# A decoder trunk in split float32: operand starts at one remainder by 256 bytes, and a gate projection in columns of 512, 512 and 320

## The chip, the core and the metric

The kernel runs on one core of a Trainium2 chip. The metric is the time of one execution on the device in microseconds (us). Each kernel is run several times, and the median is compared. Beside the runs one execution is profiled; its trace gives every instruction's start, and the views quoted here come from it.

## What is computed

The reference is a trunk of two layers over 256 tokens of width 1024, all in float32. Each layer is a half-step SwiGLU FFN, a token mixer and a second half-step FFN, each with a norm before and after. The mixer of the first layer is a gated linear recurrence (RG-LRU), that of the second is attention with a forget gate. Keys, values and forget gates come from the stream between the two layers.

```python
D_MODEL, SEQ, D_FF, D_RNN = 1024, 256, 2816, 1344

def swiglu(x, w_gate, w_up, w_down):
    return (jax.nn.silu(x @ w_gate) * (x @ w_up)) @ w_down

def recurrent_block(x, w_in, conv_w, conv_b, w_a, b_a, w_x, b_x, lam, w_out):
    gx = x @ w_in
    gate, rec = gx[..., :D_RNN], gx[..., D_RNN:]
    rec = causal_depthwise_conv(rec, conv_w, conv_b)
    rec = rg_lru(rec, w_a, b_a, w_x, b_x, lam)
    return (jax.nn.gelu(gate) * rec) @ w_out

for layer in range(2):
    if layer == 1:
        k, v, c = shared_kv(h, kv_norm_g, w_kv, w_f, b_f)     # c: running sum of the forget gates' logs
    h = h + 0.5 * rms_norm(swiglu(rms_norm(h, ...), ...), ...)
    h = h + rms_norm(recurrent_block(...) if layer == 0 else forgetting_attention(...), ...)
    h = h + 0.5 * rms_norm(swiglu(rms_norm(h, ...), ...), ...)
```

## The kernel before

**Products.** Each float32 product is made of three: both operands are split into an upper part (`whi`, `xhi`: a rounded copy) and a lower part (`wlo`, `xlo`: the rest), and `mm3` (lines 181 to 183) issues upper with upper, upper with lower, lower with upper into one accumulator. In `mm3` the tokens stand still (128 x 128, loaded into the array) and the weights move past them, up to 512 columns at a time. The 256 tokens are two halves of 128, called t = 0 and 1.

**Weights.** They come in units of up to 1024 numbers per partition. A unit is loaded into one of five `raw` tiles, split by ScalarE (`whi`, L171) and VectorE (`wlo`, L175) into one of nine pairs of tiles, and used by both halves. A unit of a projection holds two or more blocks of 128 input rows side by side: block j begins at column j times nn of the tile, nn being the width of its column group. So where a block begins in memory depends on nn.

**Stages and order.** The stages are: FFN 1 of layer 0, the recurrent mixer, FFN 2 of layer 0, keys and values together with FFN 1 of layer 1, attention, FFN 2 of layer 1. TensorE's instructions keep the order in which the program writes them: lists of units that `run` walks through for both halves, and a written-out order for the mixer (`RG_ORDER`) and the attention (`ATT_ORDER`). The other engines' instructions are ordered by a scheduler from priorities and estimated costs, except where `keep_in_program_order` holds one. `tick`, called after each unit, prepares units ahead by a planner's clock (`pace`, which counts columns) and works off deferred steps.

**FFN.** Gate and up projections have column groups of 512 (five) and 256 (one of each, in one unit). Their product, `prod`, is transposed on TensorE (L508) and split into `hhi` and `hlo`, tiles of 22 x 128 numbers per half, which are the standing operand of the down projection: 22 blocks of 128 rows, two groups of 512 columns.

**The mixer's gate.** The gate half of `w_in`, 1344 columns, is computed with the tokens standing, in three column groups (`GCOLS`): 504, 504 and 336. The groups follow the recurrence's tiles of 126 channels, four tiles to a group. `add_gate_unit` makes the units: four of two blocks each for the first two groups, three of up to three blocks for the third. When a group is complete for a half, an activation takes it out of the accumulator into a `tok` tile (L644 with the gelu at once for the first, L646 as a copy for the others); four `tok` buffers serve the six pieces in turn. `batch` later applies the gelu to the copied pieces (L800), and `gate_T` transposes them by tiles of 126 channels (L818), four tiles of group g for batch g.

**Memory.** Tiles lie in pools, which stand one behind the other in each partition's memory. A tile begins at a multiple of 32 bytes. The pools `const`, `w`, `h` and `small` stay for the whole program, and in them every `raw`, `whi`, `wlo`, `xhi` and `xlo` tile begins at a remainder of 160 by 256. Behind them lie in turn: `rgw` and the first FFN's pool `ffn_a` (160); `rgw` and the mixer's pool `rg` (160); and from the second FFN on the pool `kv`, which begins at byte 147,616 (160) and stays, with `ffn_b`, then `att`, then `ffn_c` behind it, each from byte 174,944 (96). The FFN's tiles `sil`, `prod`, `hhi` and `hlo`, and the attention's `oh` and `ol`, have sizes that are multiples of 256 bytes, so they all have their pool's remainder. `zhi` and `zlo`, the normed tokens of keys and values, lie in the place of `hhi` and `hlo`.

The functions that the change touches and their callers follow.

Of the kernel before, what the change touches and what calls it, by code (L numbers as in the profile page):

```python
# [9 lines left out]
F32 = mybir.dt.float32  # L10
F32R = mybir.dt.float32r
BF16 = mybir.dt.bfloat16
AF = mybir.ActivationFunctionType
# [3 lines left out]
P = 128  # L17
# [3 lines left out]
DRNN = 1344  # L21
BLK = 84
RT = 126
NRT = 11
NH = 16
# [14 lines left out]
def width(i):  # L40
    return RT if i < 10 else BLK
# [3 lines left out]
def trunk_kernel(ctx: ExitStack, tc: tile.TileContext, A: dict, out: bass.AP):  # L45
    nc = tc.nc
# [11 lines left out]
    def nm(s):  # L58
        uid[0] += 1
        return f"{s}_{uid[0]}"  # L60

    def mmbank():
        return psum.tile([P, 512], F32, tag="mm", name=nm("mm"), bufs=4)
# [4 lines left out]
    def trbank():  # L68
        return psum.tile([P, 512], F32, tag="tr", name=nm("tr"), bufs=2)
# [71 lines left out]
    def main_x(t, k):  # L141
        return xhi[:, k, t * P:(t + 1) * P], xlo[:, k, t * P:(t + 1) * P]
# [11 lines left out]
    def load_raw(src, parts, n, pieces=1):  # L154
        v = new_raw()[:parts, :n]
        if len(src.shape) == 3:
            a, m = src.shape[1] // pieces, n // pieces
            for c in range(pieces):
                nc.sync.dma_start(v[:, c * m:(c + 1) * m].rearrange("p (a b) -> p a b", a=a),
                                  src[:, c * a:(c + 1) * a, :])  # L160
        else:
            nc.sync.dma_start(v, src)
        return v

    def split(rawv, parts, n, pieces=1, pin=False):
        u = Unit()
        hi = wpool.tile([P, 1024], F32R, tag="whi", name=nm("whi"), bufs=WB)
        lo = wpool.tile([P, 1024], F32R, tag="wlo", name=nm("wlo"), bufs=WB)
        m = n // pieces
        for c in range(0, n, m):  # L170
            up = nc.scalar.activation(hi[:parts, c:c + m], rawv[:, c:c + m], AF.Copy)  # L171
            if settled[0] or pin:
                tc.keep_in_program_order(up)
                settled[0] = False
            nc.vector.tensor_tensor(lo[:parts, c:c + m], rawv[:, c:c + m], hi[:parts, c:c + m].bitcast(F32), ALU.subtract)  # L175
        u.hi, u.lo = hi[:parts, :n], lo[:parts, :n]
        return u

    def mm3(ps, xh, xl, wh, wl, first, last):
        tensor_work(3 * wh.shape[1])  # L180
        nc.tensor.matmul(ps, xh, wh, start=first, stop=False)  # L181
        nc.tensor.matmul(ps, xh, wl, start=False, stop=False)  # L182
        nc.tensor.matmul(ps, xl, wh, start=False, stop=last)  # L183
# [358 lines left out]
    pools = {}  # L542
# [71 lines left out]
    n_ffn1 = len(items)  # L614


    GCOLS = [(0, 4 * RT), (4 * RT, 4 * RT), (8 * RT, 2 * RT + BLK)]
    rg = {}

    def w_in(c0, n, k0, kn):  # L620
        return A["rg_w_in"][0, k0 * P:(k0 + kn) * P, c0:c0 + n].rearrange("(k p) n -> p k n", p=P)

    gacc = {}
    toks = {}
    plain = []
    xcs, tt, th, yy = {}, {}, {}, {}

    def add_gate_unit(g, k0, kn):
        c0, nn = GCOLS[g]

        def prep():
            return split(load_raw(w_in(c0, nn, k0, kn), P, kn * nn), P, kn * nn)

        def work(t, u):
            if k0 == 0:
                gacc[(g, t)] = mmbank()
            ps = gacc[(g, t)][:, :nn]
            for j in range(kn):
                k = k0 + j
                mm3(ps, *main_x(t, k), u.hi[:, j * nn:(j + 1) * nn], u.lo[:, j * nn:(j + 1) * nn], k == 0, k == 7)  # L640
            if k0 + kn == 8:
                tok = toks[(g, t)] = pools["r"].tile([P, 4 * RT], F32, tag="tok", name=nm("tok"), bufs=4)
                if (g, t) == (0, 0):
                    nc.scalar.activation(tok[:, :nn], ps, AF.Gelu_apprx_tanh)  # L644
                else:
                    nc.scalar.activation(tok[:, :nn], ps, AF.Copy)  # L646
                    plain.append(tok[:, :nn])
        rg[f"g{sum(n[0] == 'g' and n[1] != 'w' for n in rg)}"] = len(items)
        items.append((prep, work))

    def tiles_of(p):
        return [2 * p, 2 * p + 1] if p < 5 else [10]

    def pw(p):
        return RT if p < 5 else BLK
# [133 lines left out]
    def batch(g):  # L789

        pairs = [p for p in (2 * g, 2 * g + 1)]
        tps, ys = {}, {}

        def roots():
            for (a, b, w) in parts_of(g):
                v = tt[g][:w, a:b, :]
                nc.scalar.activation(v, v, AF.Sqrt)
            while plain:
                v = plain.pop(0)
                tc.keep_in_program_order(nc.scalar.activation(v, v, AF.Gelu_apprx_tanh))  # L800

        def u_of(p):
            w, m = pw(p), len(tiles_of(p))
            v = tt[g][:w, 2 * (p % 2):2 * (p % 2) + m, :]
            nc.vector.scalar_tensor_tensor(v, th[p][1][:w, :m, :], -1.0, v, ALU.mult, ALU.mult)
            nc.vector.tensor_tensor(v, v, xcs[p][:w, :m, :], ALU.mult)

        def scan(p, j):
            w = pw(p)
            v = tt[g][:w, 2 * (p % 2) + j, :]  # L810
            nc.vector.tensor_tensor_scan(v, th[p][0][:w, j, :], v, 0.0, ALU.mult, ALU.add)

        def gate_T(t):
            tok = toks[(g, t)]
            tp = tps[t] = trbank()
            for j in range(len(pairs) * 2 if g < 2 else 3):
                w = width(4 * g + j)
                nc.tensor.transpose(tp[:w, j * P:(j + 1) * P], tok[:, j * RT:j * RT + w], ident)  # L818

        def product(t):  # L820
            y = ys[t] = pools["r"].tile([RT, 4, P], F32, tag="y", name=nm("y"), bufs=2)
            if t == 0:
                yy[g] = [rw.tile([P, 1024], F32R, tag="gy", name=nm("y"), bufs=6).rearrange("p (t a b) -> p t a b", t=2, a=4)
                         for _ in range(2)]
            for (a, b, w) in parts_of(g):
                tp = tps[t][:w, a * P:b * P].rearrange("p (a b) -> p a b", a=b - a)
                nc.vector.tensor_tensor(y[:w, a:b, :], tp, tt[g][:w, a:b, t * P:(t + 1) * P], ALU.mult)
                nc.scalar.activation(yy[g][0][:w, t, a:b, :], y[:w, a:b, :], AF.Copy)

        def low(t):  # L830
            yh, yl = yy[g]
            for (a, b, w) in parts_of(g):
                nc.vector.tensor_tensor(yl[:w, t, a:b, :], ys[t][:w, a:b, :], yh[:w, t, a:b, :].bitcast(F32), ALU.subtract)

        key = ("y", g)
        q = [(0.0, key, roots)]
        for p in pairs:
            s = len(tiles_of(p)) / 2
            q.append((1.3 * s, key, lambda p=p: u_of(p)))
            q += [(0.72, key, lambda p=p, j=j: scan(p, j)) for j in range(len(tiles_of(p)))]  # L840
        q.append((0.0, key, lambda: (gate_T(0), gate_T(1))))
        for t in range(2):
            q.append((0.7, key, lambda t=t: product(t)))
        for t in range(2):
            q.append((0.7, key, lambda t=t: low(t)))
        queue.extend(q)

    def parts_of(g):
        return [(0, 4, RT)] if g < 2 else [(0, 2, RT), (2, 3, BLK)]
# [35 lines left out]
    kv = {}  # L885
# [10 lines left out]
    def kv_tiles():  # L896
        lp = ctx.enter_context(tc.tile_pool(name="kv", bufs=1, reuse_waits="tile"))
        kv["kT"] = lp.tile([HA, NH, S], F32, name="kT")
        kv["v"] = [lp.tile([P, D], F32, name=f"v{t}") for t in range(2)]
        kv["lf"] = [lp.tile([P, NH], F32, name=f"lf{t}") for t in range(2)]  # L900
        kv["c"] = [lp.tile([NH, P], F32, name=f"c{t}") for t in range(2)]
        kv["bfb"] = lp.tile([P, NH], F32, name="bfb")
        for n in ("triu", "mone", "cmask"):
            kv[n] = lp.tile([P, P], F32, name=n)
# [353 lines left out]
    rw_cm.__exit__(None, None, None)  # L1258

    kv_tiles()  # L1260
    defer(20, kv_constants)
    fcm = open_pool("f", "ffn_b")
# [57 lines left out]
```

## Time and profile before

| | us |
|---|---|
| median of 3 runs | 995.11 (994.96 to 995.67) |
| the profiled execution | 994.69 |
| its span, first to last instruction | 993.0 |
| TensorE busy in it | 984.4 (99%) |
| VectorE busy | 618.5 (62%) |
| ScalarE busy | 530.5 (53%) |

The page of the profile has the busy time of each engine, the chain of work that ended last, and groups of instructions by line. The list of waits says which engine waited for what. The timeline lists instructions with their start, their length in us, engine, line, and the operands as out<-moving,standing. The windows give, for stretches of the span, their length, TensorE's busy time and count, the granted share of TensorE's clock, and the share and rate of the DMA engines. TensorE's instructions overlap: the length in a row is longer than the distance to the next start.

### The profile page before, as it was taken

How to read it: one execution, taken by the hardware profiler on the slowest of the kernel's cores; microseconds unless marked ns; L12 is line 12 of the kernel's file. 1: busy time of each engine (PE TensorE's matmuls, PEld its weight loads, DVE VectorE, ACT ScalarE, POOL GpSimd, SP SyncE). 2: the span in 40 equal slices, each digit the busy share in tenths (PEclk: the TensorE clock that was granted, in tenths of full speed). 3: DMA queues.
4: the chain of work that ended last, by engine and by line, in shares of the span. 5: the costliest groups of instructions: out<-in, count | busy, mean ns of one | idle time of the engine just before them, and what ended most of it. 6: DMA issues, size and time to landing. Idle time of an engine off the chain costs nothing.

```text
span 993.0 us, 12910 instructions
## 1 busy us (share of the span) xinstructions
PE 984.4 (99%) x4776; PEld 816.9 (82%) x4776; DVE 618.5 (62%) x792; ACT 530.5 (53%) x752; POOL 47.0 (5%) x92
## 2 busy tenths in 40 slices
PE   9999999999999999999999999999999999999997
PEld 6888888898988888888898888888888788888886
DVE  6756554668997555554686655554488876555542
ACT  7545443568886544443564444444366765444431
POOL 2400000100003000000100000000020000000000
PEclk9999999999999999999999999999999999999999
DMA  8967556465346766555567666655542467665531
GB/s 287 310 192 206 189 190 190 150 199 160 119 132 190 217 182 191 191 182 188 131 199 237 175 187 190 190 173 190 188 172 64 126 195 212 189 189 191 182 116 42
DMA packets 92645, 178.89 MB, mean 180 GB/s; under 512 B 11966, under 2 KB 32614, under 8 KB 92582
## 3 DMA queue, kind: packets, MB, share of 16 engines
q1 hardware_dynamic: 90998, 176.89, 58.0%
q10 hardware_dynamic: 752, 1.06, 0.3%
q8 instruction: 37, 0.61, 0.3%
q0 software_dynamic: 832, 0.12, 0.1%
q14 instruction: 26, 0.21, 0.1%
HBM read 176.95 MB, written 1.05 MB: 179 GB/s over the span
## 4 chain that ended last, share of the span: by engine, by line
PE 97%; issue 1%; DMA 1%; DVE 1%; ACT 0%; POOL 0%; POOLq 0%; DVEq 0%; ACTq 0%
PE mm L181 29%; PE mm L183 29%; PE mm L182 28%; PE tr L508 2%; PE gt L739 2%; PE gt L1040 1%; PE mm L188 1%; PE mm L190 1%; PE mm L189 1%; PE mm L1169 1%; PE mm L1075 1%; DMA raw<-in_ffn_w_gate_dram 1%; PE tr L1061 1%; PE gt L212 1%; PE tr L936 0%
## 5 line engine op out<-in xcount | busy, mean ns | idle before, releaser
L175 DVE TENSOR_TENSOR wlo<-raw,whi 128x1024 fp32r<-128x1024 f32 (+4 forms) x329 | 395.7, 1208 | 271.5 <-ACT whi L171 270.9
L171 ACT ACTIVATE whi<-raw 128x1024 fp32r<-128x1024 f32 (+4 forms) x329 | 341.8, 1045 | 317.1 <-PE mm L183 253.8
L181 PE MATMUL mm<-whi,xhi 128*128 128x512 f32 (+2 forms) x768 | 303.7, 395 | 0.0
L183 PE MATMUL mm<-whi,xlo 128*128 128x512 f32 (+2 forms) x768 | 298.9, 389 | 0.3 <-DVE xlo L226 0.3
L182 PE MATMUL mm<-wlo,xhi 128*128 128x512 f32 (+2 forms) x768 | 298.1, 388 | 0.0
L183 PEld LDWEIGHTS mm<-whi,xlo 128*128 128x128 f32 x768 | 144.2, 188 | 31.0 <-DVE xlo L226 0.7
L181 PEld LDWEIGHTS mm<-whi,xhi 128*128 128x128 f32 x768 | 144.3, 188 | 28.7 <-issue 1.3
L182 PEld LDWEIGHTS mm<-wlo,xhi 128*128 128x128 f32 x768 | 144.5, 188 | 27.9 <-DVE wlo L175 0.3
L181 PE MATMUL mm<-whi,hhi 128*128 128x512 f32 x352 | 138.2, 393 | 0.0
L183 PE MATMUL mm<-whi,hlo 128*128 128x512 f32 x352 | 138.0, 392 | 0.0
L182 PE MATMUL mm<-wlo,hhi 128*128 128x512 f32 x352 | 137.5, 391 | 0.0
L182 PEld LDWEIGHTS mm<-wlo,hhi 128*128 128x128 f32 x352 | 66.1, 188 | 14.3
L183 PEld LDWEIGHTS mm<-whi,hlo 128*128 128x128 f32 x352 | 66.1, 188 | 14.0
L181 PEld LDWEIGHTS mm<-whi,hhi 128*128 128x128 f32 x352 | 66.1, 188 | 13.8
L502 DVE SCALAR_TENSOR_TENSOR prod<-mm,rstd,sil 128x512 f32<-128x512 f32 (+1 forms) x48 | 33.9, 706 | 37.7 <-PE mm L183 34.0
L493 ACT ACTIVATE sil<-mm,rstd 128x512 f32<-128x512 f32 (+1 forms) x48 | 31.2, 652 | 40.6 <-PE mm L183 40.5
L196 POOL TENSOR_SCALAR nv<-ss 128x1 f32<-128x1 f32 x22 | 9.5, 432 | 722.2 <-ACT junk L203 722.2
L512 ACT ACTIVATE hhi<-tr 128x512 fp32r<-128x512 f32 (+1 forms) x48 | 26.6, 554 | 15.4 <-PE tr L508 15.3
L203 ACT ACTIVATE junk<-mm 128x512 bf16<-128x512 f32 x24 | 14.3, 597 | 32.9 <-PE mm L183 32.8
L270 DVE TENSOR_TENSOR t<-mm,gb 128x512 f32<-128x512 f32 x24 | 16.2, 689 | 24.9 <-ACT junk L203 24.8
L513 DVE TENSOR_TENSOR hlo<-tr,hhi 128x512 fp32r<-128x512 f32 (+1 forms) x48 | 30.5, 643 | 1.4
L181 PE MATMUL mm<-whi,zhi 128*128 128x340 f32 (+2 forms) x80 | 28.3, 354 | 0.0
(195 smaller groups left out, 898.0 us busy)
## 6 DMA issues: line engine op xcount, KB each, us to landing
raw<-in_ffn_w_down_dram SPq DMA_DIRECT2D x88, 512.0 KB
raw<-in_ffn_w_up_dram SPq DMA_DIRECT2D x80, 512.0 KB
raw<-in_ffn_w_gate_dram SPq DMA_DIRECT2D x78, 512.0 KB
raw<-in_rg_w_in_dram SPq DMA_DIRECT2D x20, 504.0 KB
raw<-in_rg_w_out_dram SPq DMA_DIRECT2D x10, 504.0 KB
raw<-in_ffn_w_gate_dram SPq DMA_DIRECT2D x18, 256.0 KB
raw<-in_ffn_w_up_dram SPq DMA_DIRECT2D x16, 256.0 KB
raw<-in_w_kv_dram SPq DMA_DIRECT2D x8, 512.0 KB
```

Of the source, the lines that this page charges most:

```text
L171: up = nc.scalar.activation(hi[:parts, c:c + m], rawv[:, c:c + m], AF.Copy)
L175: nc.vector.tensor_tensor(lo[:parts, c:c + m], rawv[:, c:c + m], hi[:parts, c:c + m].bitcast(F32), ALU.subtract)
L181: nc.tensor.matmul(ps, xh, wh, start=first, stop=False)
L182: nc.tensor.matmul(ps, xh, wl, start=False, stop=False)
L183: nc.tensor.matmul(ps, xl, wh, start=False, stop=last)
L270: nc.vector.tensor_tensor(t1[n], pf[n], gb[:, n * 512:(n + 1) * 512], ALU.mult)
L493: nc.scalar.activation(s[:, :nn], ps, AF.Silu, scale=rs[t][:, 0:1])
L502: nc.vector.scalar_tensor_tensor(pr[:, :nn], ps, rs[t][:, 0:1], s, ALU.mult, ALU.mult)
L508: nc.tensor.transpose(tp[:, j * P:(j + 1) * P], pr[:, j * P:(j + 1) * P], ident)
L512: nc.scalar.activation(hv, tp[:, :nn], AF.Copy)
L513: nc.vector.tensor_tensor(lv, tp[:, :nn], hv.bitcast(F32), ALU.subtract)
L739: nc.tensor.matmul(ps[j][:w, g * S:(g + 1) * S], wv[rows, o:o + w], xc[rows, k, :], start=start, stop=stop, skip_group_check=True)
```

## The change

Three edits. The gate's column groups become 512, 512 and 320. A half's gate tokens are held in one tile of 1344 columns, of which the pieces are slices, and `gate_T` reads batch g's channels from column 504 g of it; there is one such tile for each half, `tok0` and `tok1`, in place of four buffers. And the two tiles `lf` of the pool `kv` are allocated with 8 more columns, which are not used: 96 bytes instead of 64 each, so that the pools behind `kv` begin 64 bytes later.

```diff
-    GCOLS = [(0, 4 * RT), (4 * RT, 4 * RT), (8 * RT, 2 * RT + BLK)]
+    GCOLS = [(0, 512), (512, 512), (1024, DRNN - 1024)]
...
             if k0 + kn == 8:
-                tok = toks[(g, t)] = pools["r"].tile([P, 4 * RT], F32, tag="tok", name=nm("tok"), bufs=4)
+                if t not in toks:
+                    toks[t] = pools["r"].tile([P, DRNN], F32, name=f"tok{t}")
+                tok = toks[t][:, c0:c0 + nn]
                 if (g, t) == (0, 0):
-                    nc.scalar.activation(tok[:, :nn], ps, AF.Gelu_apprx_tanh)
+                    nc.scalar.activation(tok, ps, AF.Gelu_apprx_tanh)
                 else:
-                    nc.scalar.activation(tok[:, :nn], ps, AF.Copy)
-                    plain.append(tok[:, :nn])
+                    nc.scalar.activation(tok, ps, AF.Copy)
+                    plain.append(tok)
...
         def gate_T(t):
-            tok = toks[(g, t)]
+            tok = toks[t][:, 4 * g * RT:]
...
-        kv["lf"] = [lp.tile([P, NH], F32, name=f"lf{t}") for t in range(2)]
+        kv["lf"] = [lp.tile([P, NH + 8], F32, name=f"lf{t}")[:, :NH] for t in range(2)]
```

## The prediction

> **What bounds the kernel now.** I read the page first (span, the chain of waits), then TensorE's waits, then the timeline of single products in stretches where nothing but products runs, and last the windows over those stretches with their counts.
>
> ```profile
> span 993.0 us, 12910 instructions
> PE 97%; issue 1%; DMA 1%; DVE 1%; ACT 0%; POOL 0%; POOLq 0%; DVEq 0%; ACTq 0%
> ```
>
> ```profile
> PE mm L1169 <- DVE whi L1136: 0.9, 1, 0.9
> PE tr L125 <- PEq L1305: 0.8, 1, 0.8
> PE mm L183 <- DVE xlo L226: 0.3, 1, 0.3
> PE gt L739 <- issue: 0.3, 1, 0.3
> PE mm L1169 <- ACT whi L1138: 0.2, 1, 0.2
> ```
>
> The chain of what ended last is TensorE for 97%, and TensorE's list of waits holds 2.5 us in all, 1.9 of it in the first stretch of the program (L125 and L1169 are its opening lines). So the end is set by how fast TensorE steps from one product to the next. A busy time of "0.39" in the rows below is a modelled latency: the pace is the distance from one start to the next.
>
> Here are two down projections, each in one of the stretches where only products run: the first FFN, then the second.
>
> ```profile
> 147.11 0.39 PE L181 MATMUL mm<-whi,hhi 128*128 128x512 f32 x1
> 147.34 0.39 PE L182 MATMUL mm<-wlo,hhi 128*128 128x512 f32 x1
> 147.57 0.39 PE L183 MATMUL mm<-whi,hlo 128*128 128x512 f32 x1
> 147.79 0.39 PE L181 MATMUL mm<-whi,hhi 128*128 128x512 f32 x1
> ```
>
> ```profile
> 446.32 0.39 PE L181 MATMUL mm<-whi,hhi 128*128 128x512 f32 x1
> 446.55 0.39 PE L182 MATMUL mm<-wlo,hhi 128*128 128x512 f32 x1
> 446.77 0.39 PE L183 MATMUL mm<-whi,hlo 128*128 128x512 f32 x1
> 447.01 0.39 PE L181 MATMUL mm<-whi,hhi 128*128 128x512 f32 x1
> ```
>
> The same three products, in the same shapes, take 0.68 us in the first FFN and 0.69 in the second. Whole stretches with their counts make that firm. The rows are the four down projections in order, each from its last transposes to its end (the count holds three instructions too many in each, the tail of what ran just before):
>
> ```profile
> 140.89:191.31 50.42, 50.42 (x225) 1.00 0.51 156
> 439.36:487.51 48.15, 48.15 (x213) 1.00 0.55 165
> 674.63:722.77 48.14, 48.14 (x213) 1.00 0.54 175
> 933.06:986.46 53.40, 53.40 (x236) 1.00 0.30 99
> ```
>
> 50.42 / 222 = 227.1 ns for one product in the first; 48.15 / 210 = 229.3, 48.14 / 210 = 229.2 and 53.40 / 233 = 229.2 in the others. The granted clock is 1.00 in all four. The DMA share (0.51, 0.55, 0.54, 0.30) does not order them: the last has the least traffic and the slow pace.
>
> What does order them is where the operands lie. Adding up tile sizes in the order of the pools, all weight tiles, xhi and xlo begin at remainder 160 (bytes, modulo 256). The pool of the first FFN does so too, and its hhi and hlo are whole multiples of 256 long: 160 against 160. The pool `kv` begins at 160 and holds 16384 + 2 x 4096 + 2 x 64 + 2 x 512 + 64 + 3 x 512 bytes, which is 106 x 256 + 192. So every pool opened after it begins at 96: hhi, hlo, zhi, zlo, oh, ol and their like of the later stages lie at 96 while the moving weights lie at 160.
>
> **The change part by part.** I work against the profiled execution, 994.69 us (span 993.0 and 1.69 around it); the median of the runs shown, 995.11, is 0.42 above it, and I add that at the end.
>
> *The padding of lf.* Two tiles grow from 64 to 96 bytes, so the later pools begin 64 bytes on, at 160. No instruction is added. A down projection has 22 x 2 x 2 x 3 = 264 products; three of the four move from 96 to 160: 792 x (229.25 - 227.1) = 1.70 us less. The other products with a stationary operand at 96 are the K projection (L181 to L183 with zhi, zlo) and the output projection of the attention (oh, ol), 96 products each:
>
> ```profile
> 538.53 0.47 PE L181 MATMUL mm<-whi,zhi 128*128 128x512 f32 x1
> 548.23 0.38 PE L936 MATMUL tr<-ident,htok 128*128 128x128 f32 x2
> 562.30 0.48 PE L181 MATMUL mm<-whi,xhi 128*128 128x512 f32 x1
> 571.93 0.49 PE L508 MATMUL tr<-ident,prod 128*128 128x128 f32 x3
> 795.18 0.39 PE L182 MATMUL mm<-wlo,oh 128*128 128x512 f32 x1
> 800.45 0.39 PE L181 MATMUL mm<-whi,xhi 128*128 128x512 f32 x1
> 805.91 0.27 PE L212 MATMUL gt<-ident,h 128*128 128x128 f32 x1
> ```
>
> Between 538.53 and 548.23 lie 42 products with z: 231.0 ns each, against 229.3 for the 42 products with x (160 against 160) from 562.30 to 571.93, which also begin behind transposes. That is 1.7 x 96 = 0.16 us. The 23 products with oh and ol up to 800.45 take 229.1 each, the 24 with x that follow without a break 227.5: 1.6 x 96 = 0.15 us. The V projection has 144 products of width 360 and 340, whose second slots stay at other remainders: I take nothing, bounds 144 x 2.15 = 0.3 either way. The float32 products (gates, logits, values; 122 in the code) change remainder as well, and no row shows one of them at two: nothing, bounds 122 x 2.15 = 0.3 either way.
>
> *Gate columns 512, 512, 320.* The column sum stays 1344 and so does the count of products: 96 of 504 become 512, 48 of 336 become 320. A second slot at 504 columns lies 2016 bytes on, at remainder 128; at 512 it lies at 160 again, and 320 columns are 5 x 256 bytes.
>
> ```profile
> 206.89 0.39 PE L181 MATMUL mm<-whi,xhi 128*128 128x504 f32 x1
> 209.64 0.28 PE L188 MATMUL mm<-xhi,whi 128*126 128x256 f32 x1
> 249.74 0.32 PE L183 MATMUL mm<-whi,xlo 128*128 128x336 f32 x1
> 253.14 1.03 PE L818 MATMUL tr<-ident,tok 128*126 128x128 f32 x8
> 254.14 0.28 PE L189 MATMUL mm<-xlo,whi 128*126 128x256 f32 x1
> 259.65 0.60 PE L739 MATMUL gt<-xc,gw 126*126 126x256 f32 x2
> ```
>
> Twelve products of 504 take 2.75 us, 229.2 each: more than the 227.1 of an aligned 512. By that row a wider product is 2.1 ns cheaper: 96 x 2.1 = 0.20 less. By width alone it would be dearer: 22 products of 336 take 3.40 us, 154.5 each, so a column costs (227.1 - 154.5) / 176 = 0.41 ns, and 8 columns 96 x 3.3 = 0.32 more. I take the first, since the row is of this very product; both are bounds. For 320 I have neighbours on both sides: 47 products of 256 in 5.51 us are 117.2 each, so the slope below 336 is 37.3 / 80 = 0.47. Sixteen columns less are 6.6 to 7.5 ns: 48 x 7 = 0.34 less.
>
> The Trainium skill ("TensorE: Matmul & The Clock Gate", section "Back-to-back issue gap") gives a warm gap of N / 2.4 + 2.5 ns, from the width alone. By it 504 to 512 would cost 0.32 us, 336 to 320 would return the same, and the padding would change nothing. The four windows above disagree: one width, one clock, 227.1 and 229.2.
>
> *One tile for a half's tokens.* Six pieces in four buffers become slices of two tiles, 10,752 bytes instead of 8,064; the later pools still end below the row's end. The three pieces of a half are written by the same number of activations, and the transposes read 126 columns from the slice as before. A piece of the third group no longer waits for a buffer to come free. The loads carry the same bytes in rows of 2048 and 1280 instead of 2016 and 1344; TensorE's waits name no DMA in this stage, so I cost them at nothing. If that cover were gone, a late split would show as a wait on whi or wlo; the list has none there. The splits become 1024 and 960 elements wide for 1008, on engines that are not the bound. Nothing is queued behind a new wait unless the shared tile makes one (second rival).
>
> Sum: 1.70 + 0.16 + 0.15 + 0.20 + 0.34 = 2.55 us less. 994.69 - 2.55 = 992.1 profiled, 992.5 as a median. Nothing stands ready to take the place of this time: TensorE waits for nobody between 10 and 986 us but 0.3 us twice.
>
> **The rivals.** *Width alone.* The pace goes by the width, and the slow pace of the later stages has another cause (their neighbours, their traffic). Then the padding gives nothing and the columns +0.32 - 0.34: 995.1, no change. For it: only one down projection of four is aligned, so one stage could differ for reasons of its own. Against it: oh and x in one unbroken run, one width, 229.1 and 227.5; and 504 dearer than 512. The skill's rule above is this rival's formula.
>
> *A wait on the shared tile (the slower side).* A read of one slice of a tok tile waits for the last write to any slice of it. The transposes (L818) stand in TensorE's order right behind the products of the third group, whose copy (L646) comes later on ACT:
>
> ```profile
> 255.59 0.43 ACT L646 ACTIVATE tok<-mm 128x336 f32<-128x336 f32 x1
> 272.11 1.03 PE L818 MATMUL tr<-ident,tok 128*126 128x128 f32 x8
> 273.57 0.46 ACT L646 ACTIVATE tok<-mm 128x336 f32<-128x336 f32 x1
> ```
>
> The first eight transposes start at 253.14 and would wait until 256.02, 2.9 us; the next eight at 272.11 until 274.03, 1.9 us. TensorE's order is fixed, so all products behind them wait too: +4.8 - 2.55 = +2.3, 997.4. It decides from the point where the waits together exceed 2.55. Against it, the program already writes and reads two halves of one tile at once:
>
> ```profile
> 203.99 2.17 ACT L244 ACTIVATE xhi<-gt,gT 128x128 fp32r<-128x128 f32 x8
> 204.38 0.39 PE L182 MATMUL mm<-wlo,xhi 128*128 128x504 f32 x1
> 205.16 2.16 DVE L247 SCALAR_TENSOR_TENSOR xlo<-gt,gT,xhi 128x128 fp32r<-128x128 f32 x8 [0.41 <-ACT xhi L244]
> ```
>
> ACT writes the second half's columns of xhi until 206.16 and DVE those of xlo until 207.32, while TensorE reads the first half's at 204.38 without waiting. So waits go by the bytes touched.
>
> **How the numbers follow.** Forecast 0.81, width alone 0.10, shared tile 0.09. The forecast's own bounds: at worst 1.70 + 0.34 with nothing from z and oh, 0.32 lost on the 504s, 0.3 on V and 0.3 on float32, 1.1 less, 994.0; at best 2.55 + 0.3 + 0.3, 3.15 less, 992.0. With the 0.7 us over which the three runs shown are spread (994.96 to 995.67), half to each side and a little more: 991.3 to 994.3, which leaves out the two rivals and hardly anything else. About 0.2%, 2.0 us, is what a measurement of this kernel can tell from no change. Of the forecast's share I put 0.70 beyond that and 0.11 within it; with width alone, 0.21 within; 0.09 slower.
>
> **What would show it.** Right: the windows over the second to fourth down projections give about 227.1 ns for one product, as the first did; three products take 0.68 us; each of these stages is 264 x 2.15 = 0.57 us shorter; the gate's 512-wide products step at about 227 and the 320-wide at 147; TensorE's waits stay at about 2.5 us. Wrong: the later down projections still at 229 (width alone); the transposes at L818 with an idle gap ended by ACT tok (shared tile); a new wait on whi or wlo from the gate units on, which would say that the order on ACT and DVE has shifted.

## The result and the profile after

The changed kernel takes 992.52 us (median of 8 runs, 992.08 to 993.69) against 994.87 (8 runs): ratio 0.9976, 95% interval 0.9966 to 0.9986. It is faster by 2.35 us. Its profiled execution took 992.08.

The page of the changed kernel, span and chain of waits, and below it TensorE's list of waits (us in total, times, longest):

```profile
span 990.4 us, 12910 instructions
PE 97%; issue 1%; DMA 1%; DVE 1%; ACT 0%; POOL 0%; POOLq 0%; DVEq 0%; ACTq 0%
```

```profile
PE tr L125 <- PEq L1309: 0.8, 1, 0.8
PE gt L742 <- issue: 0.5, 1, 0.5
PE mm L1173 <- ACT whi L1142: 0.3, 1, 0.3
PE mm L183 <- DVE xlo L226: 0.3, 1, 0.3
```

The same number of instructions, the same bound, no new wait on an operand. What moved is the pace. The windows over the four down projections of the changed kernel, in order; the count again holds three instructions too many:

```profile
140.68:191.10 50.42, 50.42 (x225) 1.00 0.48 157
438.80:486.53 47.73, 47.73 (x213) 1.00 0.54 167
673.20:720.92 47.72, 47.72 (x213) 1.00 0.54 176
930.93:983.87 52.94, 52.94 (x236) 1.00 0.29 100
```

The first is as long as before, 50.42 us or 227.1 ns a product. The others are 47.73 / 210 = 227.3, 47.72 / 210 = 227.2 and 52.94 / 233 = 227.2, where they had 229.2 to 229.3. The gate's rows that answer to those of the prediction (timeline):

```profile
206.72 0.39 PE L181 MATMUL mm<-whi,xhi 128*128 128x512 f32 x1
209.45 0.28 PE L188 MATMUL mm<-xhi,whi 128*126 128x256 f32 x1
249.48 0.31 PE L183 MATMUL mm<-whi,xlo 128*128 128x320 f32 x1
252.71 0.49 PE L821 MATMUL tr<-ident,tok 128*126 128x128 f32 x3
```

Twelve products of 512 columns take 2.73 us (227.5 by these rows; 2.75 before), and 22 of 320 take 3.23 (146.8 each; 3.40 before).

Summed over all products of a stage, from start to start, in the two profiled executions (us):

| | before | after | difference | predicted |
|---|---|---|---|---|
| down projections, all four | 242.03 | 240.47 | -1.56 | -1.70 |
| gate, 504 to 512 | 22.46 | 22.54 | +0.08 | -0.20 |
| gate, 336 to 320 | 7.53 | 7.14 | -0.39 | -0.34 |
| K projection | 22.33 | 22.24 | -0.09 | -0.16 |
| attention's output projection | 23.30 | 23.22 | -0.08 | -0.15 |
| V projection | 23.11 | 23.00 | -0.11 | 0 |
| other products with x, after the opening | 489.09 | 488.71 | -0.38 | 0 |
| transposes of the gate's tokens | 2.68 | 2.85 | +0.17 | 0 |
| opening, from TensorE's first instruction to its 115th | 27.22 | 27.05 | -0.17 | 0 |

The last row matters for all comparisons below. The opening varies from run to run by more than some of the effects (27.05 to 30.33 us over the kernels of this study): by the waits for the first operands, and by the pace of its first products, which the last section shows. "Outside the opening" means the span less that stretch: 965.76 before, 963.32 after, 2.44 us less.

### The profile page after: what moved, and what is told of

Its sections match the earlier page's. It is cut to its first block, busy times and chain, and to the rows that moved or that the text cites. A ratio compares the mean times of both kernels' runs of the same rounds, so it can differ in the third digit from the quotient of the medians.

```text
span 990.4 us, 12910 instructions
## 1 busy us (share of the span) xinstructions
PE 982.4 (99%) x4776; PEld 816.5 (82%) x4776; DVE 618.6 (62%) x792; ACT 530.2 (54%) x752; POOL 47.1 (5%) x92
## 4 chain that ended last, share of the span: by engine, by line
PE 97%; issue 1%; DMA 1%; DVE 1%; ACT 0%; POOL 0%; POOLq 0%; DVEq 0%; ACTq 0%
PE mm L181 29%; PE mm L183 28%; PE mm L182 28%; PE tr L508 2%; PE gt L742 2%; PE gt L1044 1%; PE mm L188 1%; PE mm L189 1%; PE mm L190 1%; PE mm L1173 1%; PE mm L1079 1%; PE tr L1065 1%; PE gt L212 1%; DMA raw<-in_ffn_w_gate_dram 1%; PE tr L940 0%
## 5 line engine op out<-in xcount | busy, mean ns | idle before, releaser
L175 DVE TENSOR_TENSOR wlo<-raw,whi 128x1024 fp32r<-128x1024 f32 (+5 forms) x329 | 395.6, 1207 | 270.1 <-ACT whi L171 267.1
L171 ACT ACTIVATE whi<-raw 128x1024 fp32r<-128x1024 f32 (+5 forms) x329 | 341.8, 1045 | 315.5 <-PE mm L183 250.6
L181 PE MATMUL mm<-whi,xhi 128*128 128x512 f32 (+1 forms) x768 | 303.5, 395 | 0.0
L183 PE MATMUL mm<-whi,xlo 128*128 128x512 f32 (+1 forms) x768 | 298.9, 389 | 0.3 <-DVE xlo L226 0.3
L182 PE MATMUL mm<-wlo,xhi 128*128 128x512 f32 (+1 forms) x768 | 298.4, 388 | 0.0
```

## The experiments

Throughout, D is the remainder by 256 of the standing operand's start less that of the moving operand's start, in the products of `mm3`. Ratios are to the kernel before. Before, D was 0 for x and for the first FFN's hidden tokens, and -64 for the standing operands of the later stages, each against the first block of a unit; further blocks of the narrower groups stood elsewhere (the gate's second blocks of 504 columns at D = +32).

**The parts alone.** First the padding without the rest:

```diff
 (the kernel before)
-        kv["lf"] = [lp.tile([P, NH], F32, name=f"lf{t}") for t in range(2)]
+        kv["lf"] = [lp.tile([P, NH + 8], F32, name=f"lf{t}")[:, :NH] for t in range(2)]
```

> Padding of lf alone, columns and token tiles as before. Theory (the start of the standing operand against that of the moving one, modulo 256, sets the pace): the later three down projections step at 227.2 to 227.3 ns as in the changed kernel, and the time is 1.8 us below before (1.56 down projections, 0.1 each for K, V and the attention's output projection): ratio 0.9982. Rival (pace by width alone, the gain of the change lies in the gate's columns): no difference, ratio 1.000, down projections still at 229.2.

Measured: 992.56 us, ratio 0.9975 (0.9966 to 0.9985). Its windows over the second and fourth down projection:

```profile
439.32:487.05 47.73, 47.73 (x213) 1.00 0.56 167
931.38:984.32 52.94, 52.94 (x236) 1.00 0.31 100
```

The pace of the changed kernel, 227.3 and 227.2, with columns and token tiles untouched. Outside the opening it is 963.48, 2.28 us below before, where 1.8 was expected; 0.31 of it lies in products with x, which were not in that sum. So nearly the whole gain is the padding.

Then the rest without the padding:

```diff
 (the changed kernel)
-        kv["lf"] = [lp.tile([P, NH + 8], F32, name=f"lf{t}")[:, :NH] for t in range(2)]
+        kv["lf"] = [lp.tile([P, NH], F32, name=f"lf{t}") for t in range(2)]
```

> Columns 512, 512, 320 and the shared token tile, lf not padded. Theory: 0.25 us from the 96 products of 512 and 0.39 from the 48 of 320, so 0.6 us below before, ratio 0.9994, which is at the edge of what can be measured; the later down projections stay at 229.2 ns. Rival (all the gain is the columns'): 2.4 us below, ratio 0.9976. Rival (the shared tile costs a wait): above before by up to 4 us, with idle time ahead of the transposes of tok.

Measured: 994.66, ratio 0.9996 (0.9987 to 1.0005): not to be told from no change by the time. The windows stay where they were before:

```profile
439.32:487.47 48.15, 48.15 (x213) 1.00 0.55 165
932.97:986.38 53.41, 53.41 (x236) 1.00 0.31 99
```

48.15 / 210 = 229.3. Outside the opening it is 965.48, 0.28 below before: half of what was expected. The 0.39 of the narrower group is there; the 0.25 of the wider ones is not (they lose 0.08, as in the table of the stages). Idle time ahead of the transposes of tok did not appear, so the rival of a wait on the shared tile is out.

**Must the two starts agree, or is 160 a good place?** One kernel moves every standing operand by 64 bytes and leaves the weights; the other moves everything to 0.

```diff
 (x_off64, the changed kernel with)
+    hpool.tile([P, 16], F32, name="shift")
     xhi = hpool.tile([P, 8, S], F32R, name="xhi")
 (all_at_0, the changed kernel with)
     gT = cpool.tile([P, 56], F32, name="gT")
+    cpool.tile([P, 24], F32, name="shift")
```

> The changed kernel with an unused tile of 64 bytes ahead of xhi: every standing operand of the wide products (x, hidden, z, y, attention output) begins at 224, the moving weights still at 160. Theory (the two starts must agree): some 3,700 products of 340 to 512 columns lose about 2.1 ns each, 7 to 8 us slower than the changed kernel, about 1000 us, ratio to before 1.005; down projections at about 229.2. Rival A (only a standing operand below the moving one costs, as 96 under 160 did): no loss, 992.5. Rival B (something other than the addresses slowed the later stages before): no loss, 992.5.

> The changed kernel with an unused tile of 96 bytes ahead of the weight tiles: every operand of the wide products, moving and standing, begins at 0 instead of 160. Theory (they must agree, wherever they lie): 992.5 as the changed kernel, down projections at 227.2. Rival (160 is a good place of itself, or the absolute place matters): another pace, 229 or above for all wide products, up to 8 us slower; or faster, if 0 is a better place.

Measured: with D = +64 everywhere 1013.32, ratio 1.0185 (1.0171 to 1.0199), 20.8 us above the changed kernel; with all at 0, 993.23, ratio 0.9984 (0.9976 to 0.9993). The first and second down projection at D = +64:

```profile
143.64:195.53 51.89, 51.89 (x225) 1.00 0.50 153
447.51:496.59 49.08, 49.08 (x213) 1.00 0.55 162
```

and with all at 0:

```profile
141.17:191.64 50.47, 50.47 (x225) 1.00 0.51 157
439.51:487.26 47.75, 47.75 (x213) 1.00 0.56 166
```

51.89 / 222 and 49.08 / 210 are 233.7 ns, also in the first FFN, which had never been slow; 50.47 / 222 and 47.75 / 210 are 227.3 and 227.4. So the place may move as long as both move. At D = +64 the direction was as the theory had it, the size was not: 6.4 ns a product and not 2.1. The price of D = -64 had been taken for the price of any disagreement. Outside the opening the kernel at 0 is 0.70 us above the changed one, all of it in products with x (489.45 for 488.71). The same sum also moves where x and the weights stay in place: among the kernels that differ only behind `kv` it goes from 488.71 (the changed one) to 489.55 (D = 128). Why, stays open.

**Around the circle.** The padding is replaced by one unused tile of n columns behind lf, which puts the standing operands of the stages from the second FFN on at 160 + D and leaves the first FFN at D = 0 as a control in the same run.

```diff
-        kv["lf"] = [lp.tile([P, NH + 8], F32, name=f"lf{t}")[:, :NH] for t in range(2)]
+        kv["lf"] = [lp.tile([P, NH], F32, name=f"lf{t}") for t in range(2)]
+        lp.tile([P, n], F32, name="shift")      # n = 24, 8, 48, 40, 56
```

> The changed kernel, but an unused tile of 96 bytes in place of the padding puts the standing operands of the later stages at 192, 32 above the moving weights' 160. Before they stood 64 under (229.2 ns a product in the down projections), and 64 above gave 233.7. Theory (the signed difference modulo 256 sets the pace, 0 is the best point): between 227.2 and 233.7, about 230 as the gate's second slots of 504 columns (32 above) had before; 2 to 3 us above the changed kernel. Rival (any disagreement costs the same by sign): 233.7, 6 us above.

> The same with an unused tile of 32 bytes: later standing operands at 128, 32 under the moving weights. Theory (0 is the best point, the loss grows with the distance): 228 ns, about 1 us above the changed kernel. Rival (any disagreement costs the same by sign): 229.2 as at 64 under. Rival (the best point lies somewhat under 0): below 227.2 ns and below the changed kernel's time.

> The same with an unused tile of 192 bytes: later standing operands at 32, 128 away from the moving weights in either direction. Theory (period 256, the loss grows with the distance): 230 ns or more in the down projections, 3 us or more above the changed kernel. Rival (period 128): 227.2 and no loss.

> The same with an unused tile of 160 bytes: later standing operands at 0, 96 above the moving weights. Theory (loss grows with the distance, more steeply above): over 233.7 ns, 6 us or more above the changed kernel. Rival (period 128: 96 above is the same as 32 under): the value that 32 under gives, about 228.

> The changed kernel with an unused tile of 224 bytes in place of the padding: later standing operands at 64, 96 under the moving weights' 160. Of the eight differences in steps of 32 it is the one not yet seen; 0 gave 227.0 ns, 64 under 229.0, and the other five 232.4 to 234.1 (stalls left out). Theory (any disagreement costs about 6 ns, 64 under is an exception): 233 ns, span some 6 us over the changed kernel's. Rival (the cheap side lies under the weights from 64 on): 229 or between 227 and 230.

Measured, one run each: 998.37, 1001.41, 999.06, 998.86 and 999.53 us; the second of them holds 3.3 us of a slower opening (last section). The second down projection in the five, in this order:

```profile
439.32:488.41 49.09, 49.09 (x213) 1.00 0.55 162
```

```profile
442.23:491.31 49.08, 49.08 (x213) 1.00 0.55 162
```

```profile
440.20:489.07 48.87, 48.87 (x213) 1.00 0.54 163
```

```profile
439.01:488.28 49.27, 49.27 (x213) 1.00 0.54 161
```

```profile
440.05:489.13 49.08, 49.08 (x213) 1.00 0.54 162
```

| D | +32 | -32 | 128 | +96 | -96 | +64 | -64 (before) | 0 (after) |
|---|---|---|---|---|---|---|---|---|
| ns a product (window / 210) | 233.8 | 233.7 | 232.7 | 234.6 | 233.7 | 233.7 | 229.3 | 227.3 |

These are all eight differences that tiles on multiples of 32 bytes can have. Six of them cost 5.4 to 7.3 ns a product; 0 costs nothing, and -64 costs 2.0. The idea that the loss grows with the distance falls: the nearest places, 32 to either side, are as bad as the far ones. So does a period of 128 bytes: 128 away is 5.4 ns slow. By number, then, the theory's forecasts for 128, +96 and -96 hold and its reason does not; +32 went as the rival said; and for -32 none of the three expectations came true. Why -64 is cheap, no run here shows. The first down projection, the control, took 50.42 to 50.43 us in all five.

The load of the standing operand does not take longer. Instructions on hhi, minimum, median and maximum in ns, in the changed kernel and with D = +32 in three of the four down projections:

```profile
L181 PEld LDWEIGHTS mm<-whi,hhi x352: 187/188/191, 129.2 to 983.2; 128*128 128x128 f32 x176
```

```profile
L181 PEld LDWEIGHTS mm<-whi,hhi x352: 187/188/190, 129.6 to 989.4; 128*128 128x128 f32 x176
```

Each load lies beside the product before it: in a down projection it starts a few ns after that product's start in both kernels. What the two operands' starts have to do with each other inside the engine, no run here shows.

**Is -64 cheap everywhere?**

```diff
 (the changed kernel with)
+    hpool.tile([P, 48], F32, name="shift")
     xhi = hpool.tile([P, 8, S], F32R, name="xhi")
```

> The changed kernel with an unused tile of 192 bytes ahead of xhi: every standing operand of the wide products begins at 96, 64 under the moving weights, in all stages. Theory (the difference alone sets the pace, so 64 under costs 2.0 ns everywhere and not only in the later stages): 3,500 products of 512 columns by 2.0, 7 us over the changed kernel, 999.5. Rival (64 under was cheap before only for those tiles or that stage): 6 ns as with 64 over, 1013. Rival (gate and up projections do not mind 64 under): 2 us, the down projections' alone, 995.

Measured: 999.41, ratio 1.0040 (1.0025 to 1.0054). The first and second down projection:

```profile
142.84:193.75 50.91, 50.91 (x225) 1.00 0.50 156
442.69:490.84 48.15, 48.15 (x213) 1.00 0.55 165
```

50.91 / 222 and 48.15 / 210 are both 229.3: the first FFN now has the pace that the later ones had before. The products with x outside the mixer go from 488.71 to 491.93 us, 1.5 ns each. Outside the opening the kernel is 5.9 us above the changed one, which is the theory a little short; the opening added 1.45 (28.50 for 27.05). So the stage is not the reason: one D gives one pace in the down projections of the first FFN and of the later ones. The products with x lose less than the 2.0 ns.

**Start and width apart.** The 504-wide blocks of the kernel before, laid 512 apart, and the V projection's blocks laid 384 apart in the changed kernel:

```diff
 (slot504, the kernel before; the load and both splits write [:, :, :504] of [P, 2, 512])
-                mm3(ps, *main_x(t, k), u.hi[:, j * nn:(j + 1) * nn], u.lo[:, j * nn:(j + 1) * nn], k == 0, k == 7)
+                mm3(ps, *main_x(t, k), u.hi[:, j * ws:j * ws + nn], u.lo[:, j * ws:j * ws + nn], k == 0, k == 7)
 (v_slots, the changed kernel; the load and both splits write [:, :, :nn] of [P, 2, 384])
-                    mm3(ps, *z_x(t, k), u.hi[:, j * nn:(j + 1) * nn], u.lo[:, j * nn:(j + 1) * nn], k == 0, k == 7)
+                    mm3(ps, *z_x(t, k), u.hi[:, j * ws:j * ws + nn], u.lo[:, j * ws:j * ws + nn], k == 0, k == 7)
```

> The kernel before with one edit in the gate's first two groups: blocks of 504 columns lie in slots of 512, so that both blocks of a unit begin at 160; width, columns, token tiles and padding as before. In the kernel before the first blocks step at 228.0 ns (stalls over 260 left out) and the second ones, at 128, at 229.5; in the changed kernel the 512-wide ones of this stage take together 0.08 us more than the 504-wide did. Theory (start and width both count, and in the gate they cancel): the second blocks fall to 228.0, the gate's 144 products to about 29.9 us from 30.0. Rival (the start does nothing at this width, as it seems to do nothing at 340 and 360): no change, 30.0.

> The changed kernel with the V projection's blocks of 360 and 340 columns in slots of 384, so that every block begins at 160. In the changed kernel the first blocks of 340 step at 155.2 ns and the second (at 240) at 158.0; at 360 both at 163.6. Theory (start counts for narrower products as well): second blocks of 340 at 155.2, the 144 products 0.1 us less (22.9 for 23.0), below what the time can tell. Rival (at these widths the start does nothing): 23.0 again.

Measured, one run each: 994.55 and 991.82. The same twelve gate products in slot504:

```profile
206.88 0.39 PE L181 MATMUL mm<-whi,xhi 128*128 128x504 f32 x1
209.60 0.28 PE L188 MATMUL mm<-xhi,whi 128*126 128x256 f32 x1
```

2.72 us: 226.7 each by these rows, with 2.75 before. In a settled stretch, then, 504 columns that agree in their start cost the same as 512 that do; with D = +32 in every second block the twelve took 2.2 ns more each, on average. Over the whole stage the gate's 144 products fall from 29.99 to 29.84 us, as expected to within 0.1. That is less than 48 x 6 ns. The stage is not what spares them: with D = +64 for all its blocks (x_off64) the gate's 512-wide products step at 233.5 ns, 23 of them between these rows:

```profile
208.71 0.39 PE L183 MATMUL mm<-wlo,xhi 128*128 128x512 f32 x1
214.08 0.28 PE L189 MATMUL mm<-xhi,whi 128*126 128x256 f32 x1
```

In the kernel before, D alternates there from block to block; whether that is the reason, no run tests.

The first V products, 18 of 360 columns, in the changed kernel and in v_slots:

```profile
499.21 0.32 PE L181 MATMUL mm<-whi,zhi 128*128 128x360 f32 x1
502.16 0.39 PE L181 MATMUL mm<-whi,xhi 128*128 128x512 f32 x1
```

```profile
499.31 0.32 PE L181 MATMUL mm<-whi,zhi 128*128 128x360 f32 x1
502.19 0.39 PE L181 MATMUL mm<-whi,xhi 128*128 128x512 f32 x1
```

2.95 us become 2.88, 163.9 ns a product become 160.0. The V projection's 144 products go from 23.00 to 22.75 us. That is more than expected, and in another place: 0.18 us of it lies in the 48 products of 360 columns, which were expected to stay as they were, while the second blocks of 340 did not fall (158.5 ns for 158.0; that 158.0 holds two stalls of 244 and 243 ns, and without them it is 154.3, no more than the first blocks take). The K projection behind them goes from 22.24 to 22.14, though its own starts are as before. So the start counts at 360 columns too. At 320 it does not: 22 products of the gate in x_off64, at D = +64, take 3.23 us, as they do in the changed kernel at D = 0.

```profile
254.41 0.31 PE L184 MATMUL mm<-whi,xlo 128*128 128x320 f32 x1
257.64 0.49 PE L822 MATMUL tr<-ident,tok 128*126 128x128 f32 x3
```

Outside the opening v_slots takes 962.99 us for the changed kernel's 963.32, and its one time, 991.82, lies below all eight of the changed kernel's. It is the best version here, by 0.3 us that the time alone would not show.

## Why the prediction was right

The forecast was 992.5 us and the measured median 992.52. The likeliest case happened, by the mechanism that was named: the pace of the later stages' products went by the operands' starts. That the two figures meet to 0.02 us is luck. The kernel before had a median of 994.87 in the comparison and not the 995.11 that the forecast started from, so the gain was 2.35 us for 2.55. And of the 2.61 us between the two profiled executions the five terms of the sum hold 2.04; most of the rest came from terms put at nothing. Point by point:

- *The down projections at about 227.1.* Right: 227.2 to 227.3, and 1.56 us for the 1.70 forecast. The padding alone brings it, the rest alone does not.
- *K and the attention's output projection.* Right in sign, about half in size (0.09 and 0.08 for 0.16 and 0.15). The terms took a settled difference for all 96 products, but the first products behind a break (a group of another kind in between) are not faster at D = 0. Where the prediction counted 42 products of the K projection, the first eleven now take 238.9 ns each for 236.3 before, and only the 31 behind them gain, 226.8 for 229.0.
- *336 to 320.* Right: 0.39 for 0.34.
- *504 to 512.* This is the term that was mis-sized: +0.08 for -0.20. The 2.1 ns came from a settled stretch and was applied to all 96 products. In settled stretches it holds (2.73 us for 2.75 over twelve). But the gate's products stand among the recurrence's. Behind the break ahead of 224.97 us (the next two are alike) the first six 512-wide products take 335, 231, 235, 229, 233 and 231 ns, where the 504-wide took 335, 225, 229, 230, 229 and 232; and the first stretch has one more long product, 311 ns where there were 229. Why, no run here shows.
- *V and the transposes, taken as nothing.* V gained 0.11, well inside its bound. The transposes of tok lost 0.17, all of it in an issue gap behind the second eight: 0.45 us where there had been 0.28.

```profile
271.51 1.03 PE L821 MATMUL tr<-ident,tok 128*126 128x128 f32 x8
273.00 1.07 PE L742 MATMUL gt<-xc,gw 84*84 84x256 f32 x4 [0.45 <-issue]
```

- *Nothing takes the place of the time.* Right: TensorE's list of waits is 1.9 us long for 2.5.
- *Products with x, not in the sum.* They gained 0.38 us over 2124 products, 0.31 of it with the padding alone. It goes with the place of the later pools: 488.69 to 488.78 in the three kernels with the padding, 489.00 to 489.09 in the three without it, one profile each. Their own starts did not change. What did is open; tiles of other engines (sil, prod) moved with the pools.

The terms missed are each under 0.4 us and cancel in part; so the sum came out closer than its parts.

*Width alone* is refuted: with the same widths, the same clock and the same order, 227.3 and 233.7 ns stand against each other. The formula of the Trainium skill ("TensorE: Matmul & The Clock Gate", section "Back-to-back issue gap"), by which the gap follows from the width, and which the page gives for a single product by itself, disagrees with these rows: for 512 columns it works out, as an estimate, at 215.8 ns, and the runs show 227.1 to 234.6 in long stretches, by the starts. *A wait on the shared tile* did not occur: no wait on tok stands in the list.

## What to carry to other kernels

Where TensorE is the bound and its waits are short, read the distance from start to start in stretches of one kind of product, and compare stretches that do the same work: a few nanoseconds, over thousands of products, are the whole gain here. If they differ, compare where the operands begin; a few unused bytes ahead of a pool can be worth more than an edit of the work, and a change in the size of any tile ahead (a new buffer, a shorter scratch tile) can cost as much as the 2.1% between 992.52 and 1013.32 us here, without an instruction changed. And a price measured at one offset is the price of that offset: -64 was the mildest of seven.

## What the runs showed of the hardware

Products whose standing and moving float32 operands begin at one remainder by 256 bytes step at 227.1 to 227.4 ns for 512 columns; at six of the seven other remainders in steps of 32 they step at 232.7 to 234.6, at the seventh at 229.3. It is the difference that counts: at difference 0 the two places tried, 160 and 0, gave one pace. At 320 columns a difference of +64 cost nothing (146.8 ns). Offsets that are no multiple of 32 were not tried.

The opening can run at about half the pace. The kernel with D = -32 was 3.3 us behind the changed one before its first FFN was under way. Its timeline begins

```profile
6.77 0.77 PE L1174 MATMUL mm<-whi,xhi 128*128 128x512 f32 x1 [0.77 <-DVE whi L1141]
7.34 0.63 PE L1174 MATMUL mm<-whi,xlo 128*128 128x512 f32 x1
7.76 0.63 PE L1174 MATMUL mm<-whi,xhi 128*128 128x512 f32 x1
8.19 0.63 PE L1174 MATMUL mm<-wlo,xhi 128*128 128x512 f32 x1
```

and that of the changed kernel

```profile
5.62 0.47 PE L1173 MATMUL mm<-whi,xhi 128*128 128x512 f32 x1
5.93 0.40 PE L1173 MATMUL mm<-whi,xlo 128*128 128x512 f32 x1
6.17 0.39 PE L1173 MATMUL mm<-whi,xhi 128*128 128x512 f32 x1
```

One product steps every 0.43 us there and every 0.24 here. In the windows from 5.60 to 12.40 us stand 17 instructions against 33 (the changed kernel second), and both rows give the granted clock as 1.00:

```profile
5.60:12.40 6.80, 6.03 (x17) 1.00 1.04 388
```

```profile
5.60:12.40 6.80, 6.52 (x33) 1.00 1.04 372
```

Here the 1.00 is no reading of the clock. The trace of the changed kernel has its first record of a granted clock at 5.49 us and that of D = -32 at 12.88, and the column counts time without a record as full. The products turn at that record: with D = -32 from 427 ns a step to 239 at 12.88, and with D = -64 everywhere, where the first record begins at 9.92, from 427 to 232 by 10.09. So the slow pace goes with the time before the first grant of the full clock. The Trainium skill ("TensorE: Matmul & The Clock Gate", section "Part 1: The HAM clock gate") describes a half clock after idleness and a window that runs free of the kernel, so that the number of slow products varies from run to run; the steps of 427 ns and the start of the records fit that. For a comparison of 2 us in 995 it means that the opening has to be taken out of a single run before its time is read.
